# A two-layer encoder trunk on one core: remainders moved to GpSimd, the convolution's sums to PSUM, the first layer's opening reordered

## The chip, the cores and the metric

The kernel runs on one core of one Trainium2 chip. The metric is the device time of one execution in microseconds, as the median of several runs.

## The reference

A trunk of two post-norm layers over 256 frames of 2048 channels, all in float32, after one layer norm of the input. Each layer mixes with attention and a convolution beside it, out of one input projection, and ends in an MLP with a squared ReLU:

```python
def hybrid_layer(x, ...):
    z = x @ w_in                                    # 2048 -> 512 + 256 + 64 + 2048
    c_q, c_kv, k_rope, u = z[..., :o1], z[..., o1:o2], z[..., o2:o3], z[..., o3:]
    q = (rms_norm(c_q, g_q) @ w_uq)                 # 8 heads of 128 + 64 (rope)
    kv = (rms_norm(c_kv, g_kv) @ w_ukv)             # 8 heads of 128 (keys) + 128 (values)
    k_rope = apply_rope(k_rope, cos, sin)           # one for all heads
    attn = chunk_causal_mla(q_nope, q_rope, k_nope, k_rope, v)
    u = u + b_glu
    h = u[..., :CONV_WIDTH] * jax.nn.sigmoid(u[..., CONV_WIDTH:])
    h = causal_depthwise_conv(h, w_dw, b_dw)        # 31 taps, 1024 channels
    h = jax.nn.silu(layer_norm(h, g_cln, b_cln))
    mix = jnp.concatenate([attn, h], axis=-1) @ w_out
    x = layer_norm(ALPHA * x + mix, ln1_g, ln1_b)
    f = jnp.square(jax.nn.relu(x @ w1)) @ w2        # 2048 -> 8192 -> 2048
    return layer_norm(ALPHA * x + f, ln2_g, ln2_b)
```

## The kernel before

All weights are read once, in chunks of 1 MB (four k-tiles of 128 rows by 512 columns; the `zk` chunks are 320 columns wide, the key and value chunks two k-tiles by 1024). `load_next` issues a chunk's transfer on SP's queue, and `cutting` splits it into two parts that TensorE multiplies at full rate: ScalarE rounds the chunk `wr` to `wh` (L249), and VectorE, or GpSimd for the chunks in `POOL_LO`, subtracts to get the remainder `wl` (L250), in two pieces of 128x1024, or four of 128x512 in the opening. The activations are split in the same way. A product is then three matmuls (high by high, low by high, high by low) into one PSUM bank: `stat_w` holds the weights still and writes channels by frames, `stat_x` holds the activations still and writes frames by channels.

`chunk_order` fixes the order of the chunks: `u` group 0, `zq`, `u` 1, `zk`, `u` 2, `qr`, `qn`, `kn`, `v`, `qn`, `u` 3, the output projection `wo` in two halves (rows of the attention, then rows of the convolution), then the MLP. `get` cuts a set number of chunks ahead of the one in use (`ahead`, mostly 2), and `retire` gives back its slots. `wr`, `wh`, `wl` and all large activations take turns on 20 slots of 128x2048 in SBUF; a slot given back is handed to the next tile that asks.

Eight PSUM banks stand in rings: four for projections (`psum`), three for transposes, scores and the like (`psumx`), one for the convolution (`psumc`). For the MLP two banks of the other rings are lent to the first.

Each `u` group (256 of the 1024 channels) ends in a gate on ScalarE and VectorE, and then its part of the convolution: for each of two blocks of 128 channels, 30 VectorE operations add a shifted and scaled `hg` to an accumulator `cv` (L618), one accumulator in PSUM and one in SBUF. They carry a low priority; `tick` emits them as far as a planned clock of VectorE allows. The convolution has to end (`flush`) before its norm (`conv_norm`), which stands after half of the first `wo` half. Attention goes by pairs of heads: scores into PSUM, their maximum and its scaling `nm` on VectorE, the exponent on ScalarE, the reciprocal `ri` and the scaling of `pr` on VectorE, transposes, and the product with the values. Both rms norms take a power on GpSimd (`rstd_of`, L343).

A planner orders each engine's instructions by priority and by its own costs when the program is built. Each engine then works its list in order and waits on semaphores.

The opening: `X` is loaded in eight pieces, two chunks in 128 KB pieces, then two whole ones, all on SP. Tile by tile `X` is normalised, transposed, scaled and offset by the input norm's `g` and `b` (on ScalarE, or on VectorE for the tiles in `GV`) and split; the cut of the first chunk, on GpSimd, is emitted after the first tile. `prepare` then loads the parameters and the taps, transposes them, computes the rope angles on GpSimd in the slot `tab`, and the tables `sinT` and `cosT` on ScalarE, all emitted before the first projection. The scale and offset of `X` itself, for the residual, are 16 GpSimd operations emitted before `u` 1 (`rest`).

## Time and profile before

| | |
|---|---|
| median of three runs | 2068.5 us (2068.22 to 2069.84) |
| the profiled execution | 2070.16 us, of which 2068.4 us span |
| TensorE busy | 1999.6 us (97%) |
| weight loads of TensorE busy | 1712.9 us (83%) |
| VectorE busy | 1359.2 us (66%) |
| ScalarE busy | 935.3 us (45%) |
| GpSimd busy | 210.0 us (10%) |
| read from HBM | 373.88 MB, 182 GB/s over the span |

PE stands for TensorE's matmuls, PEld for its weight loads, DVE for VectorE, ACT for ScalarE, POOL for GpSimd, SP for the engine that issues the transfers. Line 86 is a helper that records nearly all TensorE and VectorE operations, so a row is told apart by its tiles, written `out<-in`; L249 and L250 are the two steps of a cut, L481 is `rest`. Matmuls overlap, so the duration of one is longer than the step from one to the next. The bracket at the end of a row says how long the engine had been idle and who ended that.

### The profile page before, as it was taken

Reading aid. Unit: us, or ns where it says so; the run is one execution under the profiler, and the core shown is the slowest. Engines: PE = TensorE matmul, PEld = TensorE weight load, DVE = VectorE, ACT = ScalarE, POOL = GpSimd, SP = SyncE. Lnnn points to the kernel's source line nnn. Section 1 sums busy time; section 2 is a strip of 40 time slices with the busy share of each in tenths; the row PEclk is TensorE's granted clock in tenths of the full one; section 3 lists DMA queues with packets and bytes.
Section 4 is the critical chain, followed back from the end, with each engine's and each line's share of the span. In section 5 each row is a group of like instructions: output and inputs, shape, how many; then the busy total and the mean of one; then the engine's idle time right before and its main releaser. Section 6 shows DMA issues by size and latency. Waiting matters only on the chain. (4 is left out here: it accounts for less than half of the span.)

```text
span 2068.4 us, 26102 instructions
## 1 busy us (share of the span) xinstructions
PE 1999.6 (97%) x10518; PEld 1712.9 (83%) x10518; DVE 1359.2 (66%) x1826; ACT 935.3 (45%) x1295; POOL 210.0 (10%) x152
## 2 busy tenths in 40 slices
PE   6899899999999999999999998999999999999997
PEld 5799687888888888888879986788888888888886
DVE  5899977655555555456569998866555555555564
ACT  5445454543444444345344543555434434444441
POOL 6422412000000000000020133010000000000001
PEclk9999999999999999999999999999999999999999
DMA  7465364656645645657556535546565566566561
GB/s 240 143 186 164 122 217 149 200 188 195 212 163 191 221 157 187 204 179 249 178 165 178 158 113 197 176 153 198 186 221 163 184 201 205 163 198 220 184 228 65
DMA packets 225304, 377.66 MB, mean 183 GB/s; under 512 B 15858, under 2 KB 69986, under 8 KB 223904
## 3 DMA queue, kind: packets, MB, share of 16 engines
q1 hardware_dynamic: 225120, 375.99, 56.0%
q8 instruction: 82, 1.34, 0.3%
q14 instruction: 38, 0.31, 0.0%
q10 hardware_dynamic: 64, 0.02, 0.0%
HBM read 373.88 MB, written 2.10 MB: 182 GB/s over the span
## 5 line engine op out<-in xcount | busy, mean ns | idle before, releaser
L86 DVE TENSOR_TENSOR wl<-wr,wh 128x1024 fp32r<-128x1024 f32 (+1 forms) x648 | 771.5, 1231 | 447.4 <-ACT wh L249 309.1
L249 ACT CAST wh<-wr 128x1024 fp32r<-128x1024 f32 (+2 forms) x700 | 684.7, 1031 | 738.9 <-DVE wl L86 355.3
L86 PE MATMUL f<-xTa,wh 128*128 128x512 f32 x1920 | 676.8, 397 | 0.0
L86 PE MATMUL w<-wh,h 128*128 128x512 f32 x2048 | 631.9, 389 | 0.0
L86 PE MATMUL f<-xTa,wl 128*128 128x256 f32 x1920 | 538.0, 281 | 0.0
L86 PEld LDWEIGHTS w<-wh,h 128*128 128x128 f32 x2048 | 384.4, 188 | 80.0
L86 PEld LDWEIGHTS f<-xTa,wh 128*128 128x128 f32 x1920 | 360.4, 188 | 87.6
L86 PE MATMUL w<-wl,h 128*128 128x512 f32 x1024 | 398.4, 389 | 0.0
L86 PEld LDWEIGHTS f<-xTa,wl 128*128 128x128 f32 x1920 | 362.7, 189 | 0.9
L86 DVE SCALAR_TENSOR_TENSOR cv<-hg,wdT,cv 128x255 f32<-128x255 f32 (+21 forms) x480 | 240.1, 557 | 5.3 <-ACT cv L612 5.1
L86 PEld LDWEIGHTS w<-wl,h 128*128 128x128 f32 x1024 | 192.2, 188 | 39.6
L343 POOL TENSOR_TENSOR rb<-vb,mhalf 128x1 f32<-128x1 f32 x4 | 4.2, 1050 | 1393.7 <-DVE nmub L86 1393.7
L250 POOL TENSOR_TENSOR wl<-wr,wh 128x1024 fp32r<-128x1024 f32 (+1 forms) x52 | 112.4, 2185 | 225.3 <-ACT wh L249 124.4
L86 PE MATMUL wo<-wh,mx 128*128 128x512 f32 x256 | 87.1, 413 | 6.4 <-DVE mx L86 5.4
L86 DVE TENSOR_TENSOR X<-X,w 128x512 f32<-128x512 f32 x48 | 32.8, 688 | 72.7 <-PE w L86 72.7
L86 PE MATMUL wo<-wh,mc 128*128 128x512 f32 x256 | 79.9, 391 | 0.0
L86 PE MATMUL u<-xTi,wh 128*128 128x256 f32 x384 | 74.2, 293 | 0.0
L86 PE MATMUL u<-xTb,wh 128*128 128x256 f32 x384 | 71.3, 287 | 0.0
L86 PEld LDWEIGHTS wo<-wh,mx 128*128 128x128 f32 x256 | 50.1, 197 | 18.4 <-DVE mx L86 6.7
L86 PEld LDWEIGHTS u<-xTi,wh 128*128 128x128 f32 x384 | 63.3, 201 | 0.2
L86 PEld LDWEIGHTS u<-xTb,wh 128*128 128x128 f32 x384 | 60.8, 194 | 0.2
L86 PE MATMUL u<-xTi,wl 128*128 128x256 f32 x192 | 56.5, 294 | 0.0
(395 smaller groups left out, 1818.9 us busy)
## 6 DMA issues: line engine op xcount, KB each, us to landing
wr<-in_w_dram SPq DMA_DIRECT2D x256, 1024.0 KB, 5.2
wr<-in_w_out_dram SPq DMA_DIRECT2D x32, 1024.0 KB, 5.3
wr<-in_w_in_dram SPq DMA_DIRECT2D x60, 512.0 KB, 5.0
wr<-in_w_in_dram SPq DMA_DIRECT2D x8, 1024.0 KB, 6.8
wr<-in_w_uq_dram SPq DMA_DIRECT2D x24, 256.0 KB, 4.6
wr<-in_w_in_dram SPq DMA_DIRECT2D x8, 640.0 KB
wr<-in_w_ukv_dram SPq DMA_DIRECT2D x8, 512.0 KB, 4.5
X<-in_x_dram SPq DMA_DIRECT2D x8, 256.0 KB, 3.5
```

The costliest lines, as they stand in the source:

```text
L86: return f(*args, **kw)
L249: nc.scalar.copy(hi[:, c], raw[:, c])
L250: eng.tensor_sub(lo[:, c], raw[:, c], hi[:, c].bitcast(F32))
L343: nc.gpsimd.tensor_tensor(out=r, in0=v, in1=mhalf, op=ALU.pow)
```

## The change

It does the following:

- `gpsimd_low` takes the place of the lists: in layer 0 the remainders of `u` 2 and 3, in layer 1 of `u` 1 to 3, and in both those of `zk`, `qr`, `qn`, `kn`, `v` and the attention's half of `wo` are computed on GpSimd (58 chunks with the four of the opening, where 22 were).
- Both accumulators of the convolution lie in PSUM. The rings become three banks for projections, three for transposes and scores, two for the convolution.
- The matmuls of a chunk go through one bank and then the other (`b`, or `t` outside `ki`), with finer ticks; the first `wo` half takes its banks one by one.
- In the attention `nm` and the scaling of `pr` go from VectorE to ScalarE.
- In the opening 24 matmuls of zeros run on TensorE, the first half of `X` is loaded on two queues, two of the first chunk's four pieces are cut ahead of the first tile, and a part of that tile's scaling goes to VectorE.
- Positions, frequencies, parameters and taps are loaded among the first chunks; their transposes and the angles (now in a work tile, not in a slot) come after the first projection, the rope tables after `u` 1.
- The scale and offset of `X` is done in four rounds of four GpSimd operations, each with its own two transfers of 256 KB, before `u` 2, in `keys`, after `values`, and before `u` 3.

```diff
-POOL_U = ((2, 3), (3, 0))
-POOL_O = ((0, 0), (0, 1), (1, 0), (1, 1), (2, 0), (2, 1), (3, 1))
-POOL_LO = {("u", 0, 0, kc) for kc in range(4)} | {("u", l, i, kc) for l in range(L) for i, kc in POOL_U} | {
-    ("wo", l, 0, n, kc) for l in range(L) for n, kc in POOL_O}
-
-GV = ((1, 0), (1, 1), (0, 2))
+WARM = 24
+
+
+def gpsimd_low(key):
+
+
+    tag, l = key[:2]
+    if tag == "u":
+        return key[2] >= 2 - l or (l, key[2]) == (0, 0)
+    return tag in ("zk", "qr", "qn", "kn", "v") or (tag == "wo" and key[2] == 0)
+
+
+
+GV = {(t, n, k) for t, n in ((1, 0), (1, 1), (0, 2)) for k in range(4)} | {(0, 0, 2), (0, 0, 3)}
...
-    banks = dict(mm=[0, 1, 2, 3], ax=[4, 5, 6], cv=[7])
-
-    def bank(name, ring):
+    banks = dict(mm=[0, 1, 2], ax=[3, 4, 5])
+    CV = (6, 7)
...
+    def lend():
+
+        banks["ax"].remove(5)
+        banks["mm"][:0] = [5, *CV]
+
+    def give_back():
+        for i in (5, *CV):
+            banks["mm"].remove(i)
+        banks["ax"].append(5)
...
-        eng = nc.gpsimd if plan[i][0] in POOL_LO else vector
+        eng = nc.gpsimd if gpsimd_low(plan[i][0]) else vector
...
-    def stat_w(ps, hi, lo, ki, ncol, act, first, last):
-
-        for m in range(ncol // P):
-            o = v3(ps[m // 2], 2)[:, m % 2]
+    def stat_w(ps, hi, lo, ki, b, act, first, last):
+
+        for m in (2 * b, 2 * b + 1):
+            o = v3(ps[b], 2)[:, m % 2]
...
-                if (t, n) in GV:
+                if (t, n, k) in GV:
...
-        def rest(self):
-            for t in range(2):
-                for n in range(NC4):
-                    c = slice(n * 512, (n + 1) * 512)
-                    for w, op in ((self.g, ALU.mult), (self.b, ALU.add)):
-                        nc.gpsimd.tensor_tensor(out=X[:, t, c], in0=X[:, t, c], in1=w[:, c], op=op)
+        def rest(self, n):
+            c = slice(n * 512, (n + 1) * 512)
+            for name, ap, op in (("gi", self.g_ap, ALU.mult), ("bi", self.b_ap, ALU.add)):
+                w = work(f"{name}{n}", "gb", 3)
+                nc.sync.dma_start(w, ap[c].partition_broadcast(P))
+                for t in range(2):
+                    nc.gpsimd.tensor_tensor(out=X[:, t, c], in0=X[:, t, c], in1=w, op=op)
...
-        nc.sync.dma_start(X[:, 0, half(n)], x[0, 0:P, half(n)])
+        (nc.scalar if n % 2 else nc.sync).dma_start(X[:, 0, half(n)], x[0, 0:P, half(n)])
+
+    zeros = cst.tile([P, P], BF16, name="zeros")
+    nc.vector.memset(zeros, 0.0)
+    ps = psumx("warm")
+    for i in range(WARM):
+        nc.tensor.matmul(ps, lhsT=zeros, rhs=zeros.unsqueeze(1).broadcast_to([P, 4, P]), start=True, stop=True)
...
     load_next(True)
+    posi = cst.tile([P, 2], I32, name="posi")
+    invf = cst.tile([P, 32], F32, name="invf")
+    with nc.allow_non_contiguous_dma(reason="one position a partition"):
+        nc.sync.dma_start(posi, positions[0].rearrange("(t p) -> p t", p=P))
+    nc.sync.dma_start(invf, inv_freq.partition_broadcast(P))
     load_next()
     load_next()
+    prm = gbr[:NR * L, P:2 * P]
+    for l in range(L):
+        o = l * NR
+        for r0, nr, ap in ((0, 16, b_glu), (16, 8, g_cln), (24, 8, b_cln), (32, 8, b_dw)):
+            nc.sync.dma_start(prm[o + r0:o + r0 + nr, :], ap[l].rearrange("(r c) -> r c", c=P))
+    wdr = big("wdr")
+    for l in range(L):
+        nc.sync.dma_start(wdr[:CK, l * CW:(l + 1) * CW], w_dw[l])
...
     N.head(0)
+    first = cutting(4)
+    next(first)
+    next(first)
     ready_tile(0, 0)
-    for _ in cutting(4):
-        pass
+    state["gate"] = N.cut[:1]
+    beside(first)
+    state["gate"] = None
...
-    def prepare():
-
-        wdr = big("wdr")
-        tab = big("tab")
-        prm = tab[:NR * L, 0:P]
...
+    angles = v3(work("angles", "pr", 2)[:, 0:256], 4)
+
+    def parameters():
...
-        drop("wdr")
-        yield 1
+        drop("gbr", "wdr")
+
+    def angles_within_pi():
+
+        af, kk, kh, tmp = [angles[:, i] for i in range(4)]
...
-        yield 6
+
+    def rope_tables():
+        af, tmp = angles[:, 0], angles[:, 3]
...
-        acc = [psumc(f"cv{l}{i}0")[:, :S], work(f"cv{l}{i}1", "cva1", 1, S)]
+        acc = [psumc(f"cv{l}{i}{j}", j)[:, :S] for j in range(2)]
...
-    def out_part(ps, tag, l, k0, n, kc, act, last):
+    def out_part(ps, tag, l, k0, n, kc, act, last, tokens=(0, 1)):
 
         hi, lo = get(tag, l, k0, n, kc)
-        for ki in range(4):
-            for t in range(2):
+        for t in tokens:
+            for ki in range(4):
                 stat_x(ps[t], hi, lo, ki, act[kc][:, ki], t, kc == 0 and ki == 0, last and ki == 3)
-            if ki == 3:
-                retire(tag, l, k0, n, kc)
-            tick()
+                if ki % 2:
+                    if t and ki == 3:
+                        retire(tag, l, k0, n, kc)
+                    tick()
...
-        if l == 0:
-            beside(prepare())
-        bu = work(f"bu{l}", "gb", 2)
+        bu = work(f"bu{l}", "gb", 3)
...
+        if l == 0:
+            parameters()
         beside(gate0(ps))
+        if l == 0:
+            angles_within_pi()
...
-                for ki in range(4):
-                    for t in range(2):
+                for t in range(2):
+                    for ki in range(4):
...
         beside(rms_T(zq, QL, gqb, cq, f"q{l}"))
+        u_group(1)
         if l == 0:
-            N.load()
-            N.rest()
-        u_group(1)
+            rope_tables()
         zk = latents("zk", NKV, "zk")
...
         beside(key_rope())
+        if l == 0:
+            N.rest(0)
         u_group(2)
...
         keys(0)
+        if l == 0:
+            N.rest(1)
         keys(4)
         values(0)
         values(1)
+        if l == 0:
+            N.rest(2)
         queries(4)
...
-                    vector.tensor_scalar(out=nm[blk], in0=mx, scalar1=-SCALE, scalar2=None, op0=ALU.mult)
+                    nc.scalar.mul(nm[blk], mx, -SCALE)
...
-                        vector.tensor_scalar(out=pr[blk][:, j, 0:kend], in0=pr[blk][:, j, 0:kend],
-                                                scalar1=ri[blk][:, j:j + 1], scalar2=None, op0=ALU.mult)
+                        nc.scalar.activation(pr[blk][:, j, 0:kend], pr[blk][:, j, 0:kend], AF.Copy,
+                                             scale=ri[blk][:, j:j + 1])
...
         beside(attention((0, 1, 2, 3)))
+        if l == 0:
+            N.rest(3)
         u_group(3)
...
-        ps2 = [out_banks("wo", l, 0, n) for n in range(2)]
-        for n in range(2):
-            out_part(ps2[n], "wo", l, 0, n, 0, mixT, False)
+        pa, pb = out_banks("wo", l, 0, 0), [psum(f"wo{l}_0_1_0")]
+        out_part(pa, "wo", l, 0, 0, 0, mixT, False)
+        out_part(pb, "wo", l, 0, 1, 0, mixT, False, (0,))
         drop(f"qn{l}", f"kn{l}", f"vv{l}", f"qr{l}")
-        for n in range(2):
-            out_part(ps2[n], "wo", l, 0, n, 1, mixT, True)
-            for t in range(2):
-                accumulate(t, ps2[n], n, True)
+        out_part(pa, "wo", l, 0, 0, 1, mixT, True)
+        for t in range(2):
+            accumulate(t, pa, 0, True)
+        pb.append(psum(f"wo{l}_0_1_1"))
+        out_part(pb, "wo", l, 0, 1, 0, mixT, False, (1,))
+        out_part(pb, "wo", l, 0, 1, 1, mixT, True)
+        for t in range(2):
+            accumulate(t, pb, 1, True)
```

The helpers `bank`, `psum`, `psumx` and `psumc` are adapted to the new rings; `latents`, `u_group`, `keys` and `queries` get the same order of loops as `out_part`.

## Rows read from the trace of the kernel before

**Rows 1.** The chain that ended last: start us, us, what

```profile
1459.47 87.10 PE w L86 x384
```

**Rows 2.** Busy time of each engine by stretch; columns in the first line

```profile
core 0: us, PE busy (x) PEld busy (x) DVE busy (x) ACT busy (x) POOL busy (x), PEclk, DMA share, GB/s
...
14.90:36.00 21.10, 18.50 (x78) 13.86 (x78) 16.52 (x28) 14.60 (x33) 13.35 (x10) 1.00 0.69 199
36.00:61.00 25.00, 16.93 (x68) 13.35 (x68) 7.67 (x9) 12.50 (x17) 12.49 (x25) 0.80 0.70 230
...
80.80:151.00 70.20, 64.57 (x494) 64.20 (x493) 70.05 (x119) 27.59 (x49) 34.27 (x22) 0.95 0.60 171
151.00:216.30 65.30, 62.58 (x453) 59.64 (x452) 62.61 (x120) 36.17 (x65) 16.68 (x7) 0.97 0.46 146
216.30:286.50 70.20, 62.62 (x294) 50.90 (x294) 62.03 (x118) 30.18 (x60) 25.47 (x12) 0.95 0.54 188
...
1095.80:1222.60 126.80, 123.02 (x940) 120.20 (x939) 124.03 (x244) 62.54 (x111) 23.89 (x13) 0.98 0.55 157
1222.60:1296.40 73.80, 63.85 (x299) 51.75 (x299) 66.02 (x119) 31.26 (x62) 24.70 (x12) 0.91 0.51 180
```

**Rows 3.** Waits of TensorE, whole span: us in total, times, longest us

```profile
PE pT L86 <- DVE pr L86: 14.9, 8, 4.7
PE zq L86 <- DVE wl L86: 5.8, 1, 5.8
...
PE wdT L86 <- DMA wdr<-in_w_dw_dram: 2.3, 1, 2.3
```

**Rows 4.** The page's groups: count | busy us, mean ns | idle before

```profile
L86 DVE TENSOR_TENSOR wl<-wr,wh 128x1024 fp32r<-128x1024 f32 (+1 forms) x648 | 771.5, 1231 | 447.4 <-ACT wh L249 309.1
...
L86 DVE SCALAR_TENSOR_TENSOR cv<-hg,wdT,cv 128x255 f32<-128x255 f32 (+21 forms) x480 | 240.1, 557 | 5.3 <-ACT cv L612 5.1
```

**Rows 5.** Timeline of VectorE and GpSimd, layer 0: start us, us, instruction

```profile
82.74 13.52 POOL L481 TENSOR_TENSOR X<-X,gi 128x512 f32<-128x512 f32 x8
85.26 0.74 DVE L86 SCALAR_TENSOR_TENSOR cnq<-zq,rq,gq 128x512 f32<-128x512 f32 x1
...
136.79 0.21 DVE L86 TENSOR_TENSOR rbk<-zk,sinT 128x64 f32<-128x64 f32 x1
...
192.64 4.24 DVE L86 SCALAR_TENSOR_TENSOR cv<-hg,wdT,cv 128x245 f32<-128x245 f32 x11
...
205.41 4.69 POOL L250 TENSOR_TENSOR wl<-wr,wh 128x1024 fp32r<-128x1024 f32 x2 [3.97 <-PE u L86]
205.79 4.40 DVE L86 TENSOR_SCALAR pr<-pr,ri 128x128 f32<-128x128 f32 x2
...
210.91 0.60 DVE L86 TENSOR_SCALAR pr<-pr,ri 128x256 f32<-128x256 f32 x2
```

**Rows 6.** The tile `tab`: who waited for it (us, times)

```profile
  DVE wl L86: 6.2, 1
```

**Rows 7.** Timeline of TensorE in the opening

```profile
8.89 1.97 PE L86 MATMUL tri<-ident,X 128*128 128x128 f32 x8 [3.46 <-DVE X L86]
...
19.38 0.63 PE L86 MATMUL u<-wl,xTi 128*128 128x512 f32 x1
...
24.13 0.39 PE L86 MATMUL u<-wl,xTi 128*128 128x512 f32 x1
```

**Rows 8.** Groups of VectorE kept apart by shape, 0 to 330 us

```profile
L86 DVE TENSOR_SCALAR pr<-pr,ri 128x128 f32<-128x128 f32 x8 | 5.8, 768 | 0.0
...
L86 DVE TENSOR_SCALAR pr<-pr,ri 128x256 f32<-128x256 f32 x8 | 4.5, 605 | 0.0
```

**Rows 9.** Groups of GpSimd kept apart by shape, whole span

```profile
L250 POOL TENSOR_TENSOR wl<-wr,wh 128x1024 fp32r<-128x1024 f32 x36 | 90.9, 2546 | 223.8 <-ACT wh L249 122.9 <-issue 47.2 <-DMA wr<-in_w_uq_dram 37.9
```

**Rows 10.** The tile `zk` on TensorE: ns min/median/max, first and last start

```profile
L86 PE MATMUL zk<-wh,xTi x64: 309/309/312, 109.6 to 123.6; 128*128 128x320 f32 x64
```

**Rows 11.** Waits of GpSimd, whole span: us in total, times, longest us

```profile
POOL rq L343 <- DVE vq L86: 53.4, 3, 28.1
```

More of the change, by code (lines that the diff above doesn't have):

```diff
@@ L530, in hybrid_trunk @@
     wdT = cst.tile([P, L, 8, CK], F32, name="wdT")
-    posi = cst.tile([P, 2], I32, name="posi")
-    invf = cst.tile([P, 32], F32, name="invf")
     posf = cst.tile([P, 2], F32, name="posf")
@@ L536, in hybrid_trunk @@
     hpi = cst.tile([P, 1], F32, name="hpi")
-    def prepare():
-        wdr = big("wdr")
-        tab = big("tab")
-        prm = tab[:NR * L, 0:P]
-        af, kk, kh, tmp = [tab[:, P + 64 * i:P + 64 * (i + 1)] for i in range(4)]
-        ang = v3(af, 2)
-        for l in range(L):
-            o = l * NR
-            for r0, nr, ap in ((0, 16, b_glu), (16, 8, g_cln), (24, 8, b_cln), (32, 8, b_dw)):
-                nc.sync.dma_start(prm[o + r0:o + r0 + nr, :], ap[l].rearrange("(r c) -> r c", c=P))
-        for l in range(L):
-            nc.sync.dma_start(wdr[:CK, l * CW:(l + 1) * CW], w_dw[l])
-        with nc.allow_non_contiguous_dma(reason="one position a partition"):
-            nc.sync.dma_start(posi, positions[0].rearrange("(t p) -> p t", p=P))
-        nc.sync.dma_start(invf, inv_freq.partition_broadcast(P))
-        yield 2
+    angles = v3(work("angles", "pr", 2)[:, 0:256], 4)
+    def parameters():
         ps = psumx("prmT")
@@ L572, in prepare @@
         for t in range(2):
-            nc.gpsimd.tensor_scalar(out=ang[:, t], in0=invf, scalar1=posf[:, t:t + 1], scalar2=None, op0=ALU.mult)
+            nc.gpsimd.tensor_scalar(out=v3(af, 2)[:, t], in0=invf, scalar1=posf[:, t:t + 1], scalar2=None,
+                                    op0=ALU.mult)
         P1, P2, P3 = _two_pi_parts()
@@ L591, in prepare @@
         nc.scalar.activation(cosT.rearrange("p a b -> p (a b)"), tmp, AF.Sin, bias=hpi, scale=-1.0)
-        drop("tab")
     def rope(dst, src, t, nh, name):
@@ L724, in gate0 @@
             vconv.append(convolve(l, 0, hg, ca))
+        if l == 0:
+            parameters()
         beside(gate0(ps))
[L728 removed]
+        if l == 0:
+            angles_within_pi()
+        gqb = work(f"gq{l}", "gb", 3)
         nc.sync.dma_start(gqb, g_q[l].partition_broadcast(P))
[L730 removed]
+        gkb = work(f"gk{l}", "gb", 3)
         nc.sync.dma_start(gkb[:, :KL], g_kv[l].partition_broadcast(P))
@@ L780, in u_group @@
                 hi, lo = get("u", l, i, kc)
-                for ki in range(4):
-                    stat_w(ps, hi, lo, ki, 512, xT[kc][:, ki], kc == 0 and ki == 0, kc == 3 and ki == 3)
-                    if ki == 3:
-                        retire("u", l, i, kc)
-                    tick()
+                for b in range(2):
+                    for ki in range(4):
+                        stat_w(ps, hi, lo, ki, b, xT[kc][:, ki], kc == 0 and ki == 0, kc == 3 and ki == 3)
+                        if ki % 2:
+                            if b and ki == 3:
+                                retire("u", l, i, kc)
+                            tick()
             a = work(f"ua{l}{i}", "ev", 4)
@@ L853, in keys @@
             c = slice(h0 * P, (h0 + 4) * P)
-            for ki in range(2):
-                stat_w(ps, hi[:, :, c], lo[:, :, c], ki, 512, ck[:, ki], ki == 0, ki == 1)
-                if ki and h0:
+            for b in range(2):
+                for ki in range(2):
+                    stat_w(ps, hi[:, :, c], lo[:, :, c], ki, b, ck[:, ki], ki == 0, ki == 1)
+                if b and h0:
                     retire("kn", l)
@@ L876, in queries @@
             ps = [psum(f"qn{l}{h0}{j}") for j in range(2)]
-            for ki in range(4):
-                stat_w(ps, hi, lo, ki, 512, cq[:, ki], ki == 0, ki == 3)
-                if ki == 3:
-                    retire("qn", l, h0)
-                tick()
+            for b in range(2):
+                for ki in range(4):
+                    stat_w(ps, hi, lo, ki, b, cq[:, ki], ki == 0, ki == 3)
+                    if ki % 2:
+                        if b and ki == 3:
+                            retire("qn", l, h0)
+                        tick()
             for j in range(2):
@@ L973, in conv_norm @@
             for t in range(2):
-                pc = [psumc(f"cT{l}{t}{j}") if t and not j else psumx(f"cT{l}{t}{j}") for j in range(2)]
+                pc = [psumc(f"cT{l}{t}{j}", j) if t else psumx(f"cT{l}{t}{j}") for j in range(2)]
                 cs = sm.tile([P, 2, 6], F32, name=f"cs{l}{t}", tag="cs")
```

34 lines of the change are left out of this document (14 added, 20 removed).

## The prediction, made before the change was run

> **What bounds the kernel now.** I read the share of each engine first: TensorE is the one that hardly idles, so gains can only come from where its work is late or slow. The chain that ended last shows the pace it can hold: 384 matmuls of 512 columns in 87.10 us, 0.227 us each [rows 1]. In both MLP parts it holds this pace, and the change leaves them alone (six accumulator banks there before and after). So I cut the rest of the span into stages and asked each for busy time and granted clock [rows 2]. [...] That gives 2.6 and 11.5 us for the two opening stretches, 8.9, 4.6 and 10.7 for the rest of layer 0's mixer, 6.2 and 15.7 for layer 1's: 60.2 us in all, plus the 14.9 us before the first projection.
>
> Who ends TensorE's waits [rows 3]: mostly VectorE. In the mixers VectorE is busy almost without a gap (70.05 of 70.20 us, 124.03 of 126.80). But part of that is no work: `pr<-pr,ri` twice, which took 0.60 us at 210.91 and with twice the elements, took 4.40 us while GpSimd ran a pair of remainders from 205.41 on; an operation of the convolution costs 0.385 us (11 in 4.24), yet all 480 occupy 240.1 us and not 185 [rows 4, 5]. `cnq<-zq,rq,gq`, whose `zq` lies in PSUM, took 0.74 us in the middle of GpSimd's run over `X`, about what an operation of that size takes elsewhere (`wl`, twice the elements, 1.231) [rows 4, 5]. So an operation with SBUF inputs alone stands still while GpSimd works, and one with a PSUM input does not.
>
> The largest single wait of the opening, 5.8 us before `zq`, is one of storage: the remainder `wl` was written into the slot that `tab` had held, and waited 6.2 us for the rope tables on ScalarE, which waited for GpSimd [rows 3, 6].
>
> **The change part by part.**
> *Opening.* The angles leave the slot pool, so that 5.8 us wait has nothing to wait for; the taps are loaded ahead and transposed after the first projection, so the 2.3 us wait goes too. [...] Of 11.5 us I count 10.5; the rest stays for `zq`'s own transfer. The posi and invf transfers are put ahead of two chunk loads on SP's queue, and prm and the taps ahead of `zq`'s; the latter stood there before too, so no more is late than these two, priced in the lower bound. The first projection starts at 14.9 us [rows 2] and its matmuls last 0.63 us where later ones last 0.39 [rows 7]. Twenty-four matmuls of zeros run before; if they lift the clock, at most half of 14.9 to 20.3 us comes back, 2.7 us; they might also end late, since at twice 0.227 us they take 10.9 us and the first transposes came at 8.9 [rows 7]. I take 1.5. Cutting two of four pieces ahead of the first normalised tile, with half of its scaling on VectorE, takes two casts out of its way: 2 us (between 0 and 3). Together 14, from 6 (only the slot's wait goes) to 19 (2.6 + 11.5 + 2.7 + 2).
>
> *Remainders to GpSimd.* 58 chunks instead of 22, 16 more in layer 0, 20 more in layer 1. VectorE sheds two pieces of 1.231 us for each, five eighths of that for the eight `zk` chunks: 36 and 46 us [rows 4]. Both accumulators of the convolution in PSUM shed the blocked 55 us, 27 a layer. The softmax scaling on ScalarE sheds 10 us a layer (5.8 + 4.5 in layer 0) [rows 8]; ScalarE, busy for 94 of layer 0's 206 us there [rows 2], takes them in. In layer 0 VectorE's 195 us from 80.8 to 286.5 become 122. Still blocked are some 11 operations with two SBUF inputs (`hg`, the rope sums), at most a GpSimd piece of 2.55 us each [rows 9]: 28. That is 150 at most, where TensorE's own work is 206 - 24 = 182. VectorE stops being the bound.
>
> [...]
>
> *What is late next.* GpSimd now feeds TensorE. A piece takes 2.55 us, a chunk 5.1 [rows 9]; TensorE consumes a chunk of 24 matmuls of 512 columns, or 48 of 256, in 5.44. In layer 0 from `zk` on GpSimd has 42 pieces (107 us), eight small ones (13) and the four rounds on `X`, 16 operations of at most 1.69 (8 took 13.52; 27 in all): 147 of TensorE's 157 (109.6 to 286.5 less some 20 lost) [rows 2, 5, 10]. That is thin; each round stands ahead of chunks and waits for its own transfer on SP. I take 3 us of new waits in layer 0 and 1 in layer 1, where no rounds are; the bounds are 0 and 20.
> Three accumulator banks instead of four: the second half of the `u` group after `zq` needs the bank of `zq`'s first half, 2.7 us after the group starts (half a chunk). Before, its last reader ended at 86.0, so 2.5 us too late; after `zk`, whose last matmul starts at 123.6, the reader `rbk` ran at 136.8, some 10 us too late, behind convolution and a blocked operation [rows 5, 10]. With VectorE free I take 3 us a layer, from 0 to 13.
>
> *Sum.* Opening 14. Layer 0 from 80.8 to 216.3: 13.5 lost, all of it waits for VectorE and clock, less 6 of new waits and 0.5 kept: 7. From 216.3 to 286.5, 10.7 lost: the last convolution group with what interrupts it must end before its norm, and with blocking and scaling gone I count 9. Layer 1: 22 lost, new waits 4, and 8 kept because the attention chain (maximum, exponent, scaling, transposes) is still a chain: 10. Total 40. The profiled execution took 2070.2 us for a span of 2068.4, so 2030.2; the median run is 1.7 below it: **2028.5 us**.
>
> **The rivals.**
> *GpSimd paces layer 0.* The four rounds wait for transfers behind chunk loads, and the thin margin goes: layer 0's mixer gains nothing, 16 of 40 are gone, and with the banks' waits at 5 us more a total near 2047. For it: 147 of 157 us, and before the change GpSimd stood 53.4 us in order before `rq` [rows 11]. Against: two chunks are cut ahead, 10.9 us of cover.
> *Other side: GpSimd's queue stops behind its powers.* It works in order. `rq` and `rk` wait for VectorE; such waits were 28.1 us at most [rows 11], harmless with nothing behind. If in both layers `rq` and `rk` stand ahead of chunks and wait 21 us, each takes 21 - 10.9 = 10 us from TensorE and 1.7 of clock: 4 x 11.7 = 47, more than the 40, and 2075 us. It decides from waits of 19 us on; against it, VectorE is no longer full, so the inputs come sooner.
> *All waits go.* No new waits and none kept: 60.2 of losses and 3.5 at the start less 5 that nothing touches, 59: 2010.
> *It does little:* the opening's floor of 6 against both upper bounds of new waits in one layer: within 4 us of before.
>
> **How the numbers follow.** My sum 0.62 (2014 to 2044), GpSimd pacing layer 0 0.18 (2040 to 2058), all waits gone 0.09, little 0.03, GpSimd's stopped queue 0.08. The range leaves out the last two and half of the best case: 2010 to 2058. Changes of under 0.2%, 4 us, can't be told from none here; so faster 0.89, same 0.03, slower 0.08.
>
> **What would show it.** Right: `zq` follows `u` without a gap and at full clock before 48 us; the convolution's 480 operations near 190 us; GpSimd near 380 us busy (36 more chunks, eight of them small); VectorE no longer full between 81 and 286 us; waits `pT<-pr` nearly gone. Wrong: TensorE waiting for GpSimd's `wl` by more than 4 us, or for banks (`u` before its first matmul of a half, released by `cnq`, `rbk`); the slow clock back after 8 us because the pause behind the zeros is long; the wait before the first `X` transposes longer than 8.9 us. My weakest step is the new waits: the trace of before has none of them.

## The result, and the profile after

The changed kernel takes 2050.06 us (median of four runs, 2048.13 to 2052.07), the kernel before 2068.80 on the same chip: a ratio of 0.9910 (95% interval 0.9894 to 0.9925), 18.7 us faster. The forecast was 2028.5, so less than half of the 40 us came. The profiled execution took 2048.13 us for a span of 2046.3.

I take the stage marks from the views of the tiles, which give each tile's first and last matmul, and from TensorE's timeline. Differences of these marks give what each stage gained:

| stage | before, us | after, us | gain | forecast |
|---|---|---|---|---|
| start to the end of `zq`, layer 0 | 80.5 | 70.1 | 10.4 | 14 |
| to the end of the last `u` group | 135.6 | 143.8 | -8.2 | 7 |
| to the first `wo` matmul over `mc` | 70.4 | 56.3 | 14.1 | 9 |
| to the first MLP matmul | 45.6 | 48.8 | -3.2 | 0 |
| both MLPs with what follows | 1441.4 | 1444.3 | -2.9 | 0 |
| layer 1's mixer | 294.9 | 283.0 | 11.9 | 10 |

The gains add up to 22.1 us, the difference of the two profiled spans (2068.4 and 2046.3); the medians lie 18.7 apart. One stage explains most of the miss: layer 0 from `zq` to the last `u` group lost where it should have gained. The busy times by stretch, columns as in [rows 2]:

```profile
10.00:14.90 4.90, 1.49 (x8) 1.28 (x7) 4.90 (x8) 3.33 (x9) 2.08 (x3) 0.66 0.90 300
14.90:36.00 21.10, 17.76 (x73) 12.88 (x73) 18.33 (x26) 14.80 (x34) 20.24 (x18) 0.84 0.79 239
36.00:48.00 12.00, 12.00 (x62) 9.28 (x61) 5.56 (x5) 4.16 (x7) 8.81 (x18) 1.00 0.82 265
...
70.20:151.00 80.80, 69.37 (x518) 67.44 (x517) 60.20 (x141) 32.30 (x55) 63.83 (x39) 0.94 0.60 165
151.00:213.90 62.90, 60.52 (x460) 58.05 (x459) 35.54 (x81) 40.26 (x88) 39.42 (x17) 1.00 0.48 151
```

VectorE is no longer full (60.20 of 80.80 us, 35.54 of 62.90), as forecast, and TensorE still stands idle for 11.4 of 80.80 us. Its waits over the whole span say for whom (columns as in [rows 3]):

```profile
PE cTq L93 <- DVE cnq L93: 9.4, 1, 9.4
PE tri L93 <- DVE xv L93: 5.7, 3, 3.4
PE qrT L93 <- DVE rt L93: 4.8, 2, 2.4
PE wo L93 <- ACT mc L171: 3.5, 4, 1.2
...
PE w L93 <- DVE f115s L93: 1.4, 1, 1.4
```

All three waits of [rows 3] are gone (`pT<-pr` 14.9, `zq<-wl` 5.8, `wdT` 2.3). `qrT<-rt` (4.8) and `wo<-mc` (3.5) are new, and the wait before `cTq` has grown to 9.4 us. Before the change it was 3.5:

```profile
PE cTq L86 <- DVE cnq L86: 3.5, 1, 3.5
```

Two engines' timelines show where the 9.4 us come from; first VectorE and TensorE:

```profile
74.38 0.14 DVE L93 TENSOR_SCALAR vq<-ssq 128x1 f32<-128x1 f32 x1
...
85.72 0.75 DVE L93 SCALAR_TENSOR_TENSOR cnq<-zq,rq,gq 128x512 f32<-128x512 f32 x1 [7.47 <-POOL rq L358]
...
86.62 0.66 PE L93 MATMUL cTq<-ident,cnq 128*128 128x128 f32 x2 [9.41 <-DVE cnq L93]
```

and GpSimd:

```profile
58.66 3.66 POOL L497 TENSOR_TENSOR X<-X,gi 128x512 f32<-128x512 f32 x2 [9.55 <-DMA gi<-in_ln_in_g_dram]
67.15 3.88 POOL L497 TENSOR_TENSOR X<-X,bi 128x512 f32<-128x512 f32 x2 [4.83 <-DMA bi<-in_ln_in_b_dram]
75.10 3.51 POOL L497 TENSOR_TENSOR X<-X,gi 128x512 f32<-128x512 f32 x2 [4.07 <-DMA gi<-in_ln_in_g_dram]
82.67 2.48 POOL L497 TENSOR_TENSOR X<-X,bi 128x512 f32<-128x512 f32 x2 [4.07 <-DMA bi<-in_ln_in_b_dram]
85.11 0.57 POOL L358 TENSOR_TENSOR rq<-vq,mhalf 128x1 f32<-128x1 f32 x1
```

Behind its wait, from 86.6 us on, TensorE's granted clock reads 0.50 for 3.4 us more: three matmuls of `u` take 0.64 us there (from 88.1 on) and 0.36 later (from 90.4 on). By the reading 1.7 us are lost, by these steps 1.5; both are estimates (the windows, columns as above):

```profile
86.60:90.00 3.40, 3.38 (x16) 3.40 (x17) 2.97 (x7) 0.59 (x1) 1.69 (x2) 0.50 0.19 60
90.00:95.00 5.00, 5.00 (x44) 5.00 (x43) 3.61 (x9) 1.86 (x3) 2.30 (x3) 0.99 0.37 101
```

The power `rq` takes 0.57 us, and its input `vq` was there at 74.5. It stood in GpSimd's queue behind rounds on `X`, which the code issues only after `zk` but the planner had moved to 58.66 us, and these stood there for transfers of their own. The transfers in turn waited on SP for buffers that the rounds held (one row of SP's waits from 40 to 110 us):

```profile
SPq L495 <- POOL X L497: 19.1, 6, 4.0
```

The convolution and the load answer the forecast: the 480 operations occupy 187.1 us (240.1 in [rows 4]; "near 190"), GpSimd is busy for 361.6 us ("near 380").

```profile
L93 DVE SCALAR_TENSOR_TENSOR cv<-hg,wdT,cv 128x255 f32<-128x255 f32 (+14 forms) x480 | 187.1, 466 | 9.3 <-ACT cv L639 9.3
```

### The profile page after: what moved, and what is told of

It is laid out like the page before. It is cut to its first block, busy times and chain, and to the rows that moved or that the text cites. A ratio compares the mean times of both kernels' runs of the same rounds, so it can differ in the third digit from the quotient of the medians.

```text
span 2046.3 us, 26177 instructions
## 1 busy us (share of the span) xinstructions
PE 1995.7 (98%) x10542; PEld 1706.2 (83%) x10542; DVE 1235.9 (60%) x1709; ACT 949.2 (46%) x1343; POOL 361.6 (18%) x224
## 3 DMA queue, kind: packets, MB, share of 16 engines
q1 hardware_dynamic: 225696, 375.47, 56.3%
## 5 line engine op out<-in xcount | busy, mean ns | idle before, releaser
L93 DVE TENSOR_TENSOR wl<-wr,wh 128x1024 fp32r<-128x1024 f32 x576 | 686.4, 1235 | 432.7 <-ACT wh L264 299.1
L265 POOL TENSOR_TENSOR wl<-wr,wh 128x1024 fp32r<-128x1024 f32 (+2 forms) x124 | 268.2, 2187 | 92.8 <-ACT wh L264 44.4
L93 DVE SCALAR_TENSOR_TENSOR cv<-hg,wdT,cv 128x255 f32<-128x255 f32 (+14 forms) x480 | 187.1, 466 | 9.3 <-ACT cv L639 9.3
L93 PE MATMUL wo<-wh,mx 128*128 128x512 f32 x256 | 82.0, 396 | 1.1 <-ACT mx L171 1.1
L93 PEld LDWEIGHTS wo<-wh,mc 128*128 128x128 f32 x256 | 49.6, 194 | 15.0 <-ACT mc L171 4.5
L93 PEld LDWEIGHTS u<-xTb,wh 128*128 128x128 f32 x384 | 60.2, 191 | 0.2
L93 PEld LDWEIGHTS wo<-wh,mx 128*128 128x128 f32 x256 | 47.8, 188 | 11.5 <-ACT mx L171 1.5
## 6 DMA issues: line engine op xcount, KB each, us to landing
wr<-in_w_in_dram SPq DMA_DIRECT2D x8, 1024.0 KB, 10.4
```

Of the source, the lines that this page charges most:

```text
L93: return f(*args, **kw)
L265: eng.tensor_sub(lo[:, c], raw[:, c], hi[:, c].bitcast(F32))
```

## The experiments

Each run was timed beside the kernel before on its own chip. Runs of one group shared a chip. A comparison of times from two groups, or with the changed kernel, is one across chips, on which the kernel before differs by up to 1.6 us.

| group, run | median us | before | ratio (95% interval) |
|---|---|---|---|
| 1 rounds_in_place | 2039.72 | 2070.14 | 0.9852 (0.9837 to 0.9867) |
| 1 rounds_behind_rq | 2053.81 | 2070.14 | 0.9918 (0.9903 to 0.9933) |
| 1 no_rounds | 2036.43 | 2070.14 | 0.9836 (0.9819 to 0.9852) |
| 1 rounds_as_before | 2050.75 | 2070.14 | 0.9905 (0.9890 to 0.9920) |
| 2 remainders_alone | 2150.54 | 2069.16 | 1.0391 (1.0376 to 1.0407) |
| 2 one_accumulator_in_sbuf | 2134.52 | 2069.16 | 1.0314 (1.0299 to 1.0329) |
| 2 scaling_on_vector | 2054.88 | 2069.16 | 0.9930 (0.9913 to 0.9948) |
| 2 no_zeros | 2043.81 | 2069.16 | 0.9878 (0.9862 to 0.9895) |
| 3 operands_in_psum | 2029.14 | 2069.71 | 0.9806 (0.9791 to 0.9820) |
| 3 first_tile_scaled_by_scalar | 2040.06 | 2069.71 | 0.9854 (0.9837 to 0.9870) |
| 3 banks_back_later | 2038.37 | 2069.71 | 0.9848 (0.9833 to 0.9862) |
| 3 behind_rq_operands_in_psum | 2031.93 | 2069.71 | 0.9820 (0.9805 to 0.9834) |
| 4 after_operands_in_psum | 2045.21 | 2070.39 | 0.9880 (0.9863 to 0.9896) |
| 4 rope_in_psum | 2028.95 | 2070.39 | 0.9801 (0.9786 to 0.9815) |
| 4 turned_earlier | 2020.80 | 2070.39 | 0.9761 (0.9746 to 0.9776) |
| 4 turned_earlier_no_zeros | 2021.05 | 2070.39 | 0.9765 (0.9751 to 0.9780) |
| 5 turned_earlier_again | 2020.85 | 2070.29 | 0.9763 (0.9749 to 0.9776) |
| 5 turned_earlier_zeros_out | 2021.32 | 2070.29 | 0.9765 (0.9751 to 0.9778) |

### Where the rounds stand

**rounds_in_place.** `state["pool"]` is GpSimd's last power or remainder, `state["load"]` SP's last chunk load issued by then.

```diff
+                with tc.issue_after(state["pool"].ins), tc.issue_after(state["load"].ins):
-                nc.sync.dma_start(w, ap[c].partition_broadcast(P))
-                for t in range(2):
-                    nc.gpsimd.tensor_tensor(...)
+                    nc.sync.dma_start(w, ap[c].partition_broadcast(P))
+                    for t in range(2):
+                        nc.gpsimd.tensor_tensor(...)
```

> All four rounds on X stay, but each operation of a round, and its two loads, must stand on GpSimd's and SP's queues behind the remainder or power and the chunk load that the code issued just before it. Theory 1 (the power rq stands in GpSimd's queue behind the rounds, which stand there waiting for their own loads; TensorE waits 9.4 us for cnq and the clock takes 1.6 more): both powers run when vq is ready, near 74.4 us, the 9.4 us wait before cTq goes, and 11 us come back: 2039 us (2036 to 2043). Theory 2 (GpSimd has too much to do in layer 0, 20 us of rounds and 107 us of remainders): the same work only moves, waits of TensorE for wl appear instead, 2047 to 2052. Theory 3 (three accumulator banks: the second group waits for zq's bank whatever GpSimd does): the wait near 77 us stays at 5 us or more, 2046 to 2050.

2039.72 us, 10.3 below the changed kernel. GpSimd's timeline has the powers where their inputs come:

```profile
73.22 0.57 POOL L360 TENSOR_TENSOR rq<-vq,mhalf 128x1 f32<-128x1 f32 x1 [23.15 <-DVE vq L93]
78.50 0.55 POOL L360 TENSOR_TENSOR rq<-vq,mhalf 128x1 f32<-128x1 f32 x1 [4.71 <-DVE vq L93]
```

The wait before `cTq` is gone. Theory 1 holds. Theory 3 falls, since the wait near 77 us was to stay by it; for a bank (`rbk`) TensorE waits 0.3 us in all.

**no_rounds.** `rest` does nothing, so the scale and offset of the residual copy of `X` are left out.

> The scale and offset of the residual copy of X are left out (part of the computation is missing: the four rounds with their eight loads and 16 operations). It bounds what the rounds cost in any place. Theory 1: 2038 us, within 3 us of the run with the rounds held in place. Theory 2: GpSimd has 20 us less to do, so it is faster than the run in place by 8 us or more. Theory 3: 2046 to 2050.

2036.43 us, 3.3 below the rounds in place. With 20 us less work for GpSimd that is all there is, so its load (theory 2) is not the cause.

**rounds_as_before.** `N.load()` with two big slots and all 16 operations ahead of `u_group(1)`.

> Everything of the change but the four rounds: gi and bi are loaded whole into two big slots and all 16 operations on X stand ahead of the second u group, as in the kernel before. rq of the first tile then goes first, nine operations of 1.3 to 1.7 us stand between it and rq of the second tile. Theory 1: cTq still waits, for 12 to 15 us behind the second rq, less the 7 us of cover: TensorE loses 5 to 10 us there, 2044 to 2050. Theory 2: 2048 to 2054, as the remainders of zk come later by the whole block. Theory 3: 2046 to 2050.

2050.75 us, above the range of theory 1 and within that of theory 2 (2048 to 2054), and in theory 2's way: `cTq` waits only 0.5 us, but the block of 16 makes the remainders late (TensorE waits 6.6 us for `wl`, at `zk` and `u`), and `qrT` waits 3.1 us. GpSimd's work in one block does hold TensorE up, though spread out it costs little (no_rounds). Whole or in four rounds, the operations on `X` cost about the same where nothing holds them in place.

**rounds_behind_rq.** As in place, without `state["load"]`, and with `state["pool"]` set by the powers alone.

> The only edit: no operation of a round may stand ahead of the last power that the code issued before it (the two rk), on GpSimd's queue alone; the loads stay free. GpSimd then does all rounds within some 35 us, between remainders. Theory 1: as the run with the rounds held in place, 2039 us, at most 3 more if loads of rounds that wait for their buffers hold chunk loads behind them on SP. Theory 2: TensorE waits for wl between 125 and 180 us by more than 5 us in all, 2045 or more. Theory 3: no gain, 2046 to 2050.

2053.81 us. That lies in theory 2's range (2045 or more), but TensorE doesn't wait for `wl` at all, so no theory foresaw it, and it is the run that told most. `cTq` no longer waits, but TensorE stands before `qn`, for a bank that the sine product `rbq` has still to read:

```profile
PE qn L93 <- DVE rbq L93: 15.0, 1, 15.0
```

VectorE's timeline there, where `rbq` stands behind `hg`:

```profile
137.61 15.60 DVE L93 SCALAR_TENSOR_TENSOR hg<-ug,ua 128x512 f32<-128x512 f32 x1 [6.76 <-ACT ug L826]
153.85 0.49 DVE L93 SCALAR_TENSOR_TENSOR cv<-hg,wdT,cv 128x255 f32<-128x255 f32 x1 [0.64 <-ACT cv L640]
...
154.85 0.68 DVE L93 TENSOR_TENSOR rbq<-qr,sinT 128x512 f32<-128x512 f32 x1
```

and GpSimd's:

```profile
136.00 2.55 POOL L498 TENSOR_TENSOR X<-X,gi 128x512 f32<-128x512 f32 x2
138.51 9.28 POOL L265 TENSOR_TENSOR wl<-wr,wh 128x1024 fp32r<-128x1024 f32 x4
147.75 1.26 POOL L498 TENSOR_TENSOR X<-X,bi 128x512 f32<-128x512 f32 x1
148.97 2.48 POOL L498 TENSOR_TENSOR X<-X,gi 128x512 f32<-128x512 f32 x2
151.41 1.26 POOL L498 TENSOR_TENSOR X<-X,bi 128x512 f32<-128x512 f32 x1
```

`hg`, with two SBUF inputs, takes 0.69 us at its shortest in the changed kernel and with the rounds in place. Here it takes 15.60 us and ends 0.5 us after GpSimd's unbroken run does, at 153.21 against 152.67. It stood not for one GpSimd instruction but until that run ended, for nine in all.

### What is shut out

**operands_in_psum** (on the rounds in place). The sine products and the gate's tanh overwrite their PSUM source, so that `rt`, `kr` and `hg` each read one input from PSUM.

```diff
-        vector.tensor_tensor(out=b, in0=s4, in1=s, op=ALU.mult)
-        vector.tensor_tensor(out=d4[:, :, 0], in0=a[:, :, 0], in1=b[:, :, 1], op=ALU.subtract)
+        vector.tensor_tensor(out=s4, in0=s4, in1=s, op=ALU.mult)
+        vector.tensor_tensor(out=d4[:, :, 0], in0=a[:, :, 0], in1=s4[:, :, 1], op=ALU.subtract)
...
-                nc.scalar.activation(g[:, h], ps[1][:, h], AF.Tanh, ...)
+                nc.scalar.activation(ps[1][:, h], ps[1][:, h], AF.Tanh, ...)
```

> The version with the rounds held in place, but VectorE's last operations with two SBUF inputs in the projections get one input in PSUM: the tanh of the gate (read by hg), and the products with the sine of both rope sums (read by rt and kr), overwrite their own PSUM source. Theory: what is left of the forecast's gap in the mixers are operations that stand still beside GpSimd (rt took 4.3 us for two, hg 2.4, kr 1.5 each); the two waits of 2.4 us for rt and the half clock behind them go: 2031 to 2036 us. Rival: the banks are held longer and TensorE waits for them instead, or the rope chain is late by its own length: 2038 to 2042.

2029.14 us, 10.6 less than with the rounds in place, and below the range expected. Two rows of VectorE's timeline, first with the rounds in place:

```profile
144.58 4.32 DVE L93 TENSOR_TENSOR rt<-raq,rbq 128x256 f32<-128x256 f32 x2
```

then with an input in PSUM:

```profile
141.20 0.75 DVE L93 TENSOR_TENSOR rt<-raq,qr 128x256 f32<-128x256 f32 x2
```

The two waits of 2.4 us for `rt` are gone, and so is the lower clock behind the one in layer 0: it read 0.72 from 149 to 155 us and reads 1.00 from 130 to 155 now. By that reading, an estimate, 1.7 us were lost there. That is 6.5 of the 10.6 us; the rest isn't traced here. From the end of `zq` to the end of the last `u` group layer 0 now takes 127.0 us (133.0 in place, 135.6 before).

**rope_in_psum.** The same without the gate's part.

> The version with the rounds held in place, with only the rope sums (rt, kr) reading one product from PSUM; hg has two SBUF inputs as before. Theory (the gain of 10.6 us came from the two waits for rt and what they cost in clock): 2030 to 2033. Rival (hg, shut out in front of the rope on VectorE's queue, is half of it): 2034 to 2037.

2028.95 us: the rope sums are all of it. `hg` still took 2.00 us at 135.17, and TensorE didn't wait for it.

**behind_rq_operands_in_psum.** The PSUM inputs in the kernel that had taken 2053.81.

> The version with the rounds only held behind the powers, where the run took 2053.8 us and hg stood for 15.6 us while GpSimd ran on without a pause; here hg, rt and kr have one input in PSUM. Theory (an operation with two SBUF inputs is shut out for the whole unbroken run of GpSimd): hg takes 0.7 us, TensorE's 15 us wait goes: 2034 to 2040. Rival (the loads of the rounds hold chunk loads behind them on SP): 2048 or more, with TensorE waiting for wh or wl.

2031.93 us. GpSimd runs as unbroken as before, and `hg` no longer notices; VectorE, then GpSimd:

```profile
135.61 0.69 DVE L93 SCALAR_TENSOR_TENSOR hg<-u,ua 128x512 f32<-128x512 f32 x1 [9.17 <-ACT u L824]
```

```profile
134.51 2.56 POOL L498 TENSOR_TENSOR X<-X,gi 128x512 f32<-128x512 f32 x2
137.01 9.37 POOL L265 TENSOR_TENSOR wl<-wr,wh 128x1024 fp32r<-128x1024 f32 x4
```

The loads left free on SP cost at most the 2.8 us between this and operands_in_psum.

**after_operands_in_psum.** The PSUM inputs in the changed kernel itself.

> The changed kernel itself (rounds where the schedule put them), only with hg, rt and kr reading one input from PSUM. Theory (two causes that add: the rounds ahead of rq, 10 us, and the operations shut out by GpSimd, 10 us): 2038 to 2041 us, with the 9.4 us wait before cTq still there. Rival (the two overlap, since the rounds are what keeps GpSimd busy): 2044 or more.

2045.21 us: 4.9 gained (6.2 by the ratios, as the chips differ), not 10, and a wait of 10.6 us before `cTq`. The rival's range is right: the causes overlap. Perhaps, while TensorE stands before `cTq`, GpSimd gets ahead with its remainders and shuts the rope out less afterwards; that is not shown.

### The parts by themselves

**remainders_alone** (the kernel before, with one line changed):

```diff
-        eng = nc.gpsimd if plan[i][0] in POOL_LO else vector
+        eng = nc.gpsimd if gpsimd_low(plan[i][0]) else vector
```

> The kernel before with one part of the change: the 36 further chunks whose remainders GpSimd computes. The second accumulator of the convolution stays in SBUF, the scaling of the softmax on VectorE. Theory A (the sum of the prediction): VectorE sheds 82 us and what is blocked stays near 55 us, so the mixers gain: 2045 to 2060 us. Theory B (every VectorE operation with SBUF inputs alone stands still as long as GpSimd works, and GpSimd now works almost without a pause): the 480 operations of the convolution occupy more than 300 us instead of 240, and it is no faster than before: 2068 to 2095.

2150.54 us, 81 slower than before, worse than either theory said, though the convolution reached 298.2 and not over 300. Groups of VectorE (busy us, mean ns):

```profile
L93 DVE SCALAR_TENSOR_TENSOR cv<-hg,wdT,cv 128x255 f32<-128x255 f32 (+14 forms) x480 | 298.2, 688 | 13.3 <-ACT cv L619 13.1
...
L93 DVE TENSOR_SCALAR pr<-pr,ri 128x128 f32<-128x128 f32 (+1 forms) x32 | 32.0, 1040 | 0.2
```

**one_accumulator_in_sbuf** (on the rounds in place).

```diff
-        acc = [psumc(f"cv{l}{i}{j}", j)[:, :S] for j in range(2)]
+        acc = [psumc(f"cv{l}{i}0", 0)[:, :S], ca[:, 2 * i + 1]]
```

> The version with the rounds held in place, with one part of the change undone: the second accumulator of the convolution lies in SBUF again (in the tile that the result is copied to) and its bank is a fourth one for the projections. Theory A: 27 us a layer more on a VectorE that has room, and fewer waits for banks: 2038 to 2048. Theory B: the convolution occupies more than 300 us and sets the end of both mixers: 2060 or more. If the fourth bank were worth more than the blocking, it would be below 2038.

2134.52 us, 95 more, although the bank that this sets free goes to the projections. The two accumulators do the same 240 operations each, one with its sum in SBUF (`ca`), one in PSUM (`cv`):

```profile
L93 DVE SCALAR_TENSOR_TENSOR ca<-hg,wdT,ca 128x255 f32<-128x255 f32 (+14 forms) x240 | 238.5, 994 | 0.8 <-ACT ca L642 0.7
L93 DVE SCALAR_TENSOR_TENSOR cv<-hg,wdT,cv 128x255 f32<-128x255 f32 (+14 forms) x240 | 110.4, 460 | 10.9 <-ACT cv L642 10.9
```

**scaling_on_vector** (on the rounds in place): `nm` and `pr` by `vector.tensor_scalar` again.

> The version with the rounds held in place, with the softmax scaling (nm and pr) on VectorE again. Theory A (it matters only as load: 10 us a layer on an engine with room): 2038 to 2042. Theory B (pr<-pr,ri has SBUF inputs alone, stands still beside GpSimd, and the attention chain waits for it): waits of pT for pr come back with 5 to 15 us, 2045 to 2055.

2054.88 us, 15 more. It is not the load but the wait, as theory B says:

```profile
PE pT L93 <- DVE pr L93: 10.3, 7, 1.9
```

Both operations have a single tensor input, in SBUF, and are slow beside the busier GpSimd all the same: `nm`, of two elements, takes 1.21 us on average, where it took 0.157 before the change.

```profile
L93 DVE TENSOR_SCALAR nm<-mx 128x2 f32<-128x2 f32 x16 | 19.4, 1210 | 0.2
```

```profile
L86 DVE TENSOR_SCALAR nm<-mx 128x2 f32<-128x2 f32 x16 | 2.5, 157 | 0.0
```

### The opening, the change-over and the banks

**no_zeros:** `WARM = 0`, on the rounds in place.

> The version with the rounds held in place, without the 24 matmuls of zeros. The prediction gave them 1.5 us of 2.7 (half of the first projection's first 5.4 us): 2041 to 2042. Rival: the pause of 3.7 us behind the first transposes drops the clock anyway, so they bring nothing: 2039 to 2040.5, with the first projection starting at the same time.

2043.81 us on another chip, above both ranges. The opening is faster without zeros (`zq` starts at 47.8, not 49.2). Two stretches with zeros (columns as in [rows 2]):

```profile
10.00:15.00 5.00, 1.43 (x9) 1.22 (x8) 4.94 (x8) 3.33 (x9) 2.11 (x2) 0.81 0.93 301
15.00:25.00 10.00, 7.52 (x28) 5.07 (x26) 9.33 (x9) 4.94 (x11) 9.22 (x9) 0.75 0.88 266
```

and without:

```profile
10.00:15.00 5.00, 2.33 (x11) 1.96 (x10) 4.98 (x8) 3.52 (x9) 2.14 (x3) 1.00 0.92 287
15.00:25.00 10.00, 8.05 (x30) 5.38 (x29) 7.39 (x10) 5.08 (x10) 10.00 (x10) 1.00 0.86 268
```

Yet the whole was longer, in part by the wait for a bank at the last pass of the first MLP (3.0 us, 1.1 with the zeros). Whether the zeros matter stayed open until the last pair below.

**first_tile_scaled_by_scalar:** `(0, 0, 2)` and `(0, 0, 3)` leave `GV`.

> The version with the rounds held in place; the one edit is that all four columns of the first tile of X are scaled on ScalarE, none on VectorE, which has four normalisations queued ahead of them. Theory: TensorE's 3.6 us wait behind the first transposes shrinks to 1.5, the first projection starts near 12.6 us: 2037 to 2038.5. Rival: the next tile or the chunk's remainder is no earlier, and the projection only waits later: 2039 to 2041.

2040.06 us, no gain. The first projection does start at 13.5 us instead of 14.7, and then waits 2.4 us for the next `xTi`, whose remainder from two SBUF inputs took 1.63 us beside GpSimd. The rival is right.

**banks_back_later:** `give_back` returns bank 5, and the convolution's two follow behind `close`.

> The version with the rounds held in place; of the three banks lent to the MLP only the one of the transposes goes back ahead of the last closing pass, the two of the convolution behind it. Theory: the waits of TensorE for f015s and f115s at the start of that pass (1.1 and 1.2 us, three accumulator banks in rotation where there were four) go: 2037 to 2038. Rival: the wait is for the result itself, not the bank: 2039 to 2040.5.

2038.37 us. The waits for `f015s` and `f115s` are gone, and the two MLP parts of the span take 714.8 and 726.5 us, as before the change (714.8 and 726.6), where the rounds in place took 716.2 and 728.0.

**turned_earlier:** on operands in PSUM and later banks, one more edit; `turned` is the last transpose of `yT` for the second column pair.

```diff
-            ps = out_rows("wo", l, 0, n, mixT)
+            ps = out_banks("wo", l, 0, n)
+            out_part(ps, "wo", l, 0, n, 0, mixT, False)
+            with ExitStack() as order:
+                if n == 3:
+                    order.enter_context(tc.issue_after(state["turned"].ins))
+                out_part(ps, "wo", l, 0, n, 1, mixT, True)
```

> Rounds in place, operands in PSUM, banks back later, and one more edit: the last out projection chunk over the attention's half (n=3, second chunk) stands behind the transposes of yT for the first two column pairs on TensorE's queue. Theory: the pause of 3.1 us a layer between the last chunk over mx and the first over mc, where TensorE waits for the norm's last steps, goes: 2 x 3 and 1.5 for the banks less than 2029: 2021 to 2024. Rival (yt is late anyway, then the chunk waits too): 2027 to 2031.

2020.80 us, the fastest version, 49.6 below the kernel before. TensorE's timeline at the change-over without the edit (operands_in_psum), where the last `wo` over `mx` starts at 251.4:

```profile
251.66 0.60 PE L93 MATMUL yT<-ident,yt 128*128 128x128 f32 x4
253.16 0.44 PE L93 MATMUL yT<-ident,yt 128*128 128x128 f32 x2 [0.89 <-ACT zz L1042]
254.57 0.50 PE L93 MATMUL wo<-wh,mc 128*128 128x512 f32 x1 [0.98 <-ACT mc L171]
```

and with it, where the last one starts at 253.3:

```profile
244.91 0.81 PE L93 MATMUL yT<-ident,yt 128*128 128x128 f32 x6
...
252.61 0.38 PE L93 MATMUL yT<-ident,yt 128*128 128x128 f32 x2
253.52 0.40 PE L93 MATMUL wo<-wh,mc 128*128 128x512 f32 x1
```

The norm's transposes had stood behind the chunk although `yt` was ready.

**turned_earlier_no_zeros** adds `WARM = 0`, the first tile on ScalarE, and `v = ps` in `gain`.

> As the run with the transposes turned earlier, and the opening once more: no zeros, the first tile scaled on ScalarE, and the scaled tiles written over their own PSUM source, so that the remainders of X (which took 1.63 us instead of 0.69 beside GpSimd) have one input in PSUM. Theory (the opening's missing 3.5 us are the shut-out remainders and the lower clock that shows up behind the zeros): the second projection starts near 46 us instead of 49, 3 us faster than the run it builds on. Rival (the opening waits for its weights and the second half of X): within 1 us of it.

2021.05 us: within the rival's 1 us. `xTi` takes 0.67 to 0.69 us now, but in the profiled execution, the slowest of the four (2024.03), the opening waits elsewhere: `zq` starts 1.1 us earlier (48.0) and ends 2.9 later, after a pause of 1.9 us near 54.

**turned_earlier_again** and **turned_earlier_zeros_out**, one chip, the only difference `WARM`.

> The fastest version once more (zeros in, transposes turned earlier), beside the same without zeros on the same chip: 2019.5 to 2022 us.

> The fastest version, the one edit being that the 24 matmuls of zeros are left out. By the opening of the run without zeros (the second projection started 1.4 us earlier and the granted clock stayed at 1.00 where the zeros are followed by 0.75 to 0.84): 1 to 2 us faster than the version with zeros. By its total, which was 4 us longer: 1 us or more slower, then from a place behind the opening. By the prediction's term: 1.5 us slower.

2020.85 us, as expected, and 2021.32, where none of the three forecasts has it; both spans are 2019.4. Without the zeros `zq` ends 1.2 us earlier (70.1 and 71.3); where that is lost again isn't shown. On the whole the zeros are worth nothing that can be measured.

## Why the prediction was wrong, step by step

The failed step is "each round stands ahead of chunks and waits for its own transfer on SP ... I take 3 us of new waits in layer 0". The mechanism was named and its place was wrong. The prediction read the rounds' place from the code, behind `zk`; the planner put them in front of `rq`, and there their waits held TensorE for 9.4 us (3.5 stood there before) and, by the reading of 0.50 over 3.4 us, cost some 1.7 of clock behind them, where 3 had been taken. Holding the rounds in place gave back 10.3. The rival of the other side had the queue the wrong way round: not chunks behind powers that wait, but powers behind rounds that wait.

A second step failed under it: "Still blocked are some 11 operations with two SBUF inputs ..., at most a GpSimd piece of 2.55 us each". That one piece bounds such a wait was the author's estimate. In the changed kernel it held (2.56 us at most for `rt`, 2.41 for `hg`); it broke in rounds_behind_rq, where GpSimd ran longer without a pause (15.60). What failed is that they were counted as load on VectorE, where there is room, although `rt` lies on the chain to `qrT`, which waited 4.8 us for it. With the rounds in place, taking the shut-out away gave 10.6 us, all of it through the rope; in the changed kernel itself, 4.9. With both causes gone the time is 2029.14, and the stages, from the same marks, are: 8.8 (14 forecast) for the opening, 8.6 (7) to the end of the last `u`, 14.5 (9) to the convolution's half, 14.3 (10) for layer 1. That the total then meets 2028.5 is partly luck: the opening is too small, the others larger.

The other terms of the sum:

- *Losses by stage, 60.2.* They are each stretch's idle time plus (1 - granted clock) x busy [rows 2], which assumes that time is lost in step with the reading. Before the change three matmuls of 512 columns take 1.28 us where it reads 0.50 (57 to 61 us) and 0.68 where it reads 0.98 (44 to 50); but from 18.1 us on three take 1.28 as well, and there it reads 1.00. So the term is about right behind the waits, and no run shows it for the start of the first projection.
- *Opening, 14.* The slot's wait and the taps' went [rows 3], and `zq` follows `u` without a gap at clock 1.00 (36 to 48 us). Most of the 10.4, 8.3 us, lies between the first and the last matmul of `zq`, which took 30.3 us and now take 22.0. The 1.5 us for the zeros are 0 by the last pair: no run shows the half of 5.4 us that was to come back, and with the zeros the first matmuls still take 0.63 us. The sign that the prediction set against them came: the slow clock was back behind the pause of 3.4 us (0.66, then 0.84). Of the "2 us" for the two casts at most the 0.5 came by which the first projection starts earlier (14.4): TensorE waits for `xv`, and an earlier start was given back at `xTi`.
- *Banks, 3 us a layer.* Oversized in the mixers of the changed kernel: waits for a bank were 0.3 us there. Its mechanism, a reader late behind a blocked operation, came in full only in rounds_behind_rq (15.0 us). In the MLPs, which the sum had at nothing ("the change leaves them alone"), 1.1 to 1.4 us appeared at each last closing pass, which had three banks in rotation where there had been four; they went when the convolution's two banks were given back later.
- *From the last `u` to the convolution's half, 9.* 14.1 came, but a pause at the change-over to `mc` was not foreseen: `wo` waits for `mc` in each layer (3.5 us in both), and the stage to the first MLP matmul lost 3.2. The cause is the place of the norm's transposes in TensorE's queue: with them ahead of the chunk that stage takes 45.7 us again.
- *Layer 1, 10.* 11.9: right.
- *GpSimd paces layer 0, 2047.* The time came out near this rival's, and the rounds did wait for their transfers, but what they held up was a power and not the chunks (TensorE waits 1.6 us for `wl` in all). Leaving all rounds out gains only 3.3 us once they stand in place.
- *VectorE sheds 82, 55 and 20 us.* Right for the three together (`cv` 187.1 us, `pT<-pr` gone) and wrong as separate terms. Remainders alone cost 81 us, one accumulator back in SBUF 95, the scaling back on VectorE 15. The accumulators' place is no saving to be added to the move of the remainders; it is what makes that move possible. The scaling's place is worth 15 us, but without it the kernel still ends below the one before (2054.88 against 2069.16). What the other edits bring without the move of the remainders wasn't run.

On the last point, the same operation of the convolution took 994 ns on average with its sum in SBUF and 460 with it in PSUM (one_accumulator_in_sbuf), and 36 more chunks on GpSimd with nothing else of the change cost 81 us (remainders_alone). The longest shut-out measured here lasted over nine GpSimd instructions (15.60 us). The 4.40 us of `pr<-pr,ri` [rows 4, 5] are not of an operation with two tensor inputs, since `pr` is its only one, and neither is the slow `nm` (1.21 us on average, 0.157 before the change). One SBUF input alone, then, didn't keep an operation clear of GpSimd here.

## What to carry to other kernels

An instruction of half a microsecond is priced by what can stand in front of it in its engine's order (here `rq`, 0.57 us, behind rounds that cost TensorE 9.4), so look for it in the order that the planner will emit, not in the code, and hold filler work behind it. When work moves to GpSimd, list VectorE's instructions whose tensor inputs all lie in SBUF, price each at GpSimd's longest unbroken run (here 15.60 us for `hg`) and by who waits for it, and give one input to PSUM first (`hg`: 0.69 us). Parts that share such a shut-out can't be priced one by one: remainders alone were 81 us slower, and with the accumulators in PSUM, the rope's product too, two queue positions fixed and the other parts of the change, the same move ended 49.6 us faster.

## What the runs showed of the hardware that was not expected

- VectorE's `hg` stood for 15.60 us while GpSimd ran nine instructions without a pause, and took 0.69 us beside an equally unbroken run once one input lay in PSUM. Other shut-out operations got in earlier (`ca` in one_accumulator_in_sbuf: 2.63 us at most, mean 0.994); what decides between them these runs don't show.
- Before the change the granted clock reads 1.00 from 14.9 to 36 us [rows 2] while early matmuls take 0.63 us and later ones 0.39 [rows 7]. With the 24 zeros ahead, and TensorE idle for most of 10 to 13.7 us behind them (0.30 of 3.70 us busy), it reads 0.66, then 0.84 (0.50 from 14.4 to 20 us), and the first matmuls of the projection take 0.63 us all the same. So the row didn't tell the slow start of this kernel, and the zeros changed the reading without changing that time.
